# A norm's row factor multiplied after the products instead of before them, in a two-layer decoder step on one NeuronCore

## The chip, the cores and the metric

The kernel runs on one core of a Trainium2 chip. The time is the device time of one execution in microseconds (us). The engines named below are TensorE (PE, the matrix products; its weight loads are listed apart as PEld), VectorE (DVE), ScalarE (ACT), GpSimd (POOL) and SyncE (SP, which only issues transfers). ACT can issue transfers too, from a queue of its own.

## The reference, cut to what matters

One step of a decoder with two layers over 1024 prompt tokens and 8 sample tokens (1032 rows in all, d = 1024). Every layer is: norm, mixer, output projection plus residual, norm, feed-forward plus residual. Cut to what the change touches:

```python
def _rmsnorm(x, g):
    r = lax.rsqrt(jnp.mean(x * x, axis=-1, keepdims=True) + EPS)   # one factor per token (row)
    return x * r * g

# mixer A (layer 0): gate branch, RG-LRU input branch and memory queries
h = _rmsnorm(x, norm_mix_g);  z = h @ w_in_a
# output projection and residual, then the feed-forward
x = x + mix @ w_out
u = _rmsnorm(x, norm_ffn_g) @ w_ffn_up            # 1024 -> 6144: 24 pairs of 128 gate and 128 value columns
u = causal_conv3(u, state) + bias                 # along the tokens, samples from their own state
x = x + (gelu(u_gate) * u_value) @ w_ffn_down     # 3072 -> 1024
```

The norm's factor r is one number per token, so (x * g * r) @ w equals r * ((x * g) @ w).

## The kernel before, in words

Activations lie with features on the 128 partitions and tokens along the free axis. Every product is taken in three parts: both operands are split into a rounded part (hi) and a rest (lo), and `mm3` issues hi by hi, hi by lo and lo by hi. The hi comes from ACT (a copy, `acopy`, recorded at L105), the lo from a subtraction on DVE (`vtt`, L113) or on POOL (`gtt`, L116). Weights arrive on SP's queue, ACT makes hi, POOL makes lo (`get`, `w_split`), one tile ahead.

The tokens are cut into blocks of 384, 384 and 264 for the mixers and into four quarters of 258 (`QB`, `QW`) for the output projection and the feed-forward. The order on PE, DVE, POOL and SP is chosen by the Tile framework's scheduler; ACT keeps program order in layer 0 and in the feed-forward of layer 1.

In time the stages are: norm of the input and the first gate products (0 to 60 us), memory keys and queries, the RG-LRU stage (190 to 333), output projection 0 with the entry into the feed-forward (333 to 522), feed-forward up (522 to 985) and down (985 to 1245), mixer B, output projection 1 with its entry (1625 to 1785), up (1785 to 2246), down (to the end).

**Entry.** `x_norm(b)` squares the 8 feature tiles of a block, sums them with one product by `ones` each on PE (L565), takes Ln and Exp for r, and multiplies x by g and r before the split.

**Output projection.** `out_proj` goes over two halves of the tokens and in each over 8 feature tiles m: it loads the residual tile x[m] on SP (`residual`, L772), takes two quarters of 258 tokens in 24 products each, adds the result into x[m] on DVE, stores the sum to `rD` on SP (L1323), squares it on ACT and sums on DVE. After each half `norm` takes r of both quarters (`inverse`, product at L1335), multiplies all of x by g and r, and builds the differences T1 to T4 of the quarters for the feed-forward.

**Feed-forward up.** It is a Strassen-like scheme: for each pair of columns j, seven products P1 to P7 of 24 matmuls on each half of the tokens, 168 matmuls of 258 columns per j. POOL makes the combinations of the weights and their lo, ACT their hi; DVE adds the products into the row buffers ug and uv. `post(j)` then does for ug and uv: tap 2 and bias on ACT over 1032 columns, the last columns copied to `ul` on POOL (L867), two taps on DVE (L119) over 1023 and 1022 columns and an 8-column addition for the samples; then gelu on ACT, the product gate by value on DVE, and a store.

Of the kernel before, what the change touches and what calls it, by code (L numbers as in the profile page):

```python
# [34 lines left out]
QW = HALF // 2  # L35
QB = tuple(QW * q for q in range(4))
DCH = 6
NDC = KF // DCH
# [6 lines left out]
SEQUENCE = ENTRY + tuple((j, p, (0, 1)) for j in range(1, KF) for p in STEADY)  # L45
ORDER_A = ("g2", "g3", "x0", "x1", "x2", "x3", "x4", "x5", "g4", "g5")
# [3 lines left out]
def tile_trunk(ctx: ExitStack, tc: tile.TileContext, I: dict, O: list):  # L50
# [149 lines left out]
    def x_load(b):  # L200
        c0, n = BLK[b]
        per = 1024 // n if n > 264 else 3
        for k0 in range(0, KD, per):
# [3 lines left out]
            for j in range(m):  # L207
                X[b, k0 + j] = t[:, j * n : (j + 1) * n]

    x_load(0)  # L210
    pack = cst(PACK, "pack")
    ident = pack[:, 0:P]
# [340 lines left out]
    def unspill(k):  # L553
        t = row()
        SY.dma_start(t[:, :SEQ].rearrange("p (i t) -> p i t", i=8), xD[0:8, :, k, :].rearrange("i p t -> p i t"))
        SY.dma_start(t[:, SEQ:NT], xD[8, :, k, :NB])
        return t
# [132 lines left out]
    def sample_mem(l, dst):  # L690
# [35 lines left out]
        yield  # L726
        t = ps()
# [40 lines left out]
    def residual(l, m):  # L768
        if l:
            return unspill(m)  # L770
        t = row()
        SY.dma_start(t[:, :NT], I["x_t"][:, m, :])  # L772
        return t

    def out_proj(l, mget, ks, x, on_tile, on_half):
        for hb in range(2):
            for m in range(KD):
# [4 lines left out]
                for q in (2 * hb, 2 * hb + 1):  # L782
                    c0 = QB[q]
# [15 lines left out]
    def ffn_prep(l):  # L799
# [11 lines left out]
        vtt(s3, s3, c3, add)  # L811

# [45 lines left out]
    def ffn(l, x, ops, need, weights, on_block, store=None):  # L858
# [11 lines left out]
        def taps(a, u, t):  # L870
            stt(a[:, 1:SEQ], u[:, 0 : SEQ - 1], fwc(1, t), a[:, 1:SEQ], mul, add)
            stt(a[:, 2:SEQ], u[:, 0 : SEQ - 2], fwc(0, t), a[:, 2:SEQ], mul, add)
            vtt(a[:, SEQ:NT], a[:, SEQ:NT], sb3[:, :, t], add)

        def post(j):
# [9 lines left out]
            act(ag[:, :NT], ag[:, :NT], AF.Gelu_apprx_tanh)  # L885
            yield
            vtt(ag[:, :NT], ag[:, :NT], av[:, :NT], mul)
            SY.dma_start(gD[l, j], ag[:, :NT])
            yield

# [61 lines left out]

        last = []
        todo = [(0, p) for p in STEADY] + [(j, p) for j, p, _ in SEQUENCE if j]
        at = 7
        for q, (j, name, hfs) in enumerate(SEQUENCE):
            if q == 6:
                load_pair(1)
            want = 7 if q < 10 else min(len(todo), q - 7 + AHEAD)
# [51 lines left out]
        for b in range(3):  # L1011
            for m in range(KD):
                down(c, m, b)
                if store is not None:
                    store(m, b)
                tick()
            on_block(b)
# [4 lines left out]
    def x_norm(b):  # L1022
        n = BLK[b][1]
        xb = [X.pop((b, k)) for k in range(KD)]
        r = sm()
        yield from norm_r(xb, n, r[:, :n], b < 2)
        yield from norm_h(xb, b, r[:, :n], g_mix[0], hh, hl, True)

    load_w(1)
    SY.dma_start(pack, I["pack"])  # L1030
    x_load(1)
    load_w(2)
# [58 lines left out]
    def xr_dense(t, b):  # L1091
# [14 lines left out]
        def post():  # L1106
# [3 lines left out]
            acopy(u[:, 3 : 3 + n], p[:, :n])  # L1110
# [65 lines left out]
    def gt_dense(t, b):  # L1176
# [7 lines left out]
        if t == KR - 1:  # L1184
            act(M[t][:, cs], p[:, :n], AF.Gelu_apprx_tanh)
        else:
            acopy(M[t][:, cs], p[:, :n])
        if b == 2:
            drop(f"gt{t}")
            if t == KR - 1:  # L1190
                gelu_done.add(t)
            else:
                gelu_wait.append(t)
# [10 lines left out]
    x0 = start(x_norm(0))  # L1204
    ts(V, pack[:, 432:560], pack[:, 432:560], 0.125, None, mul, None)
    get("gt0", 0, 0)
    advance(x0)
    advance(x0)
    x1 = start(x_norm(1))
    finish(x0)  # L1210
    get("gt1", 0, 0)
    finish(x1)
    x2 = start(x_norm(2))
    for _ in range(3):
        advance(x2)
    tasks.remove(x2)
    gt_dense(0, 0)
    gt_dense(1, 0)
    gt_dense(0, 1)
    tasks.append(x2)  # L1220
    finish(x2)
    memt = start(mem_turn(mems))
    mems = None
    tasks.remove(memt)
    gt_dense(1, 1)
    gt_dense(0, 2)
    tasks.append(memt)
    gt_dense(1, 2)
# [23 lines left out]
    for i in range(9):  # L1252
# [10 lines left out]
        start(q_mem(0, p[:, :256], i, ready0) if i < 8 else q_sample(0, p[:NB, :256]))  # L1263
# [23 lines left out]
    SY.dma_start(O[1], yl)  # L1287
    SY.dma_start(O[2], rl)
# [21 lines left out]
    def enter_ffn(l, x, mh, ml):  # L1310
        ops, gen, sums = {}, {}, {}

        def split(name, kk, hf, pair, raw, on_pool):
            hi, lo = pair
            acopy(hi, raw)
            (gtt if on_pool else vtt)(lo, raw, f(hi), sub)
            ops[name, kk, hf] = pair

        def cols(q):
            return slice(QB[q], QB[q] + QW)  # L1320

        def on_tile(q, m):
            SY.dma_start(rD[l, m, :, cols(q)], x[m][:, cols(q)])  # L1323
            if m == 0:
                sums[q] = sm()
                act(sums[q][:, :QW], x[m][:, cols(q)], AF.Square)
            else:
                t = sm()
                act(t[:, :QW], x[m][:, cols(q)], AF.Square)
                vtt(sums[q][:, :QW], sums[q][:, :QW], t[:, :QW], add)  # L1330

        def inverse(q):
            a = sums.pop(q)
            p = ps()
            T.matmul(p[:, :QW], ones, a[:, :QW], start=True, stop=True)  # L1335
            m, out, t = sm()[:, :QW], sm()[:, :QW], sm()[:, :QW]
            ts(V, m, p[:, :QW], 1.0 / D, EPS, mul, add)
            act(out, m, AF.Ln)
            act(out, out, AF.Exp, scale=-0.5)
            stt(t, m, -0.5, out, mul, mul)  # L1340
            vtt(t, t, out, mul)
            stt(out, t, 1.5, out, add, mul)
            return out

        def norm(hf):
            qa, qb = cols(2 * hf), cols(2 * hf + 1)
            ra, rb = inverse(2 * hf), inverse(2 * hf + 1)
            yield
            xs = lambda k, part: x[k][:, part]

            def scale(k, part, r):
                stt(xs(k, part), xs(k, part), g_ffn[l][k], r, mul, mul)

            def slot(k, part):
                return mh[k][:, part], ml[k][:, part]

            def own(n):
                for i in range(n):
                    if i % 2 == 0:
                        t = row(F32R)  # L1360
                    b = (i % 2) * 2 * QW
                    yield t[:, b : b + QW], t[:, b + QW : b + 2 * QW]

            for k in range(KD):
                scale(k, qa, ra)
                split("B11" if k < 4 else "B21", k % 4, hf, slot(k, qa), xs(k, qa), k % 2)
                if k % 4 == 3:
                    yield
            t2 = own(4)
            for kk in range(4):  # L1370
                scale(kk, qb, rb)
# [620 lines left out]
```

## Time and profile before

| | us |
|---|---|
| median of 3 runs | 2532.33 (2530.51 to 2533.36) |
| the profiled execution's own time | 2532.97 |
| its span, first to last instruction | 2531.2 |
| PE busy | 2336.5 (92%) |
| DVE, ACT, POOL busy | 1549.6, 1103.5, 1428.0 |
| mean granted clock of PE | 0.964 |

Busy time of an engine holds what an instruction waits inside itself, once it has started. The idle time before an instruction names what was awaited last. A matmul's end is modelled, so the rate of PE is read from how many matmuls stand in a window rather than from one row.

### The profile page before, as it was taken

To read this page: it belongs to the slowest core of one execution; us is meant where nothing else is said; L and a number is where in the kernel's file an instruction comes from. 1 tells how busy PE (TensorE), PEld (TensorE's weight loads), DVE (VectorE), ACT (ScalarE), POOL (GpSimd) and SP (SyncE) were. 2 spreads that over 40 slices of the span, in tenths; PEclk is the share of its full clock that TensorE was granted. 3 is DMA by queue.
4 is the path that set the end of the run, shared out by engine and by line. 5 is a ranking of instruction groups with operands and counts; after the bars stand their busy time and mean duration, and the time that the engine had idled before them with its cause. 6 is when DMAs were issued, how large, how long until landed. Compare 5 with 4: busy or idle time off the path is not lost. (4 is left out here: it accounts for less than half of the span.)

```text
span 2531.2 us, 42857 instructions
## 1 busy us (share of the span) xinstructions
PE 2336.5 (92%) x16590; PEld 2251.5 (89%) x16590; DVE 1549.6 (61%) x2826; ACT 1103.5 (44%) x2277; POOL 1428.0 (56%) x1123
## 2 busy tenths in 40 slices
PE   7997877799999999999989988787999999999999
PEld 5896866799999999999977787677999999999999
DVE  6658955666666666332478789875666566663321
ACT  5567753344433444211365577643443444442110
POOL 2149843588888885322144346435888888853220
PEclk9998989899999999999999999899999999999999
DMA  4221124212222225421575543551222222253311
GB/s 163 87 69 56 58 83 143 63 67 84 84 85 76 76 76 199 150 95 52 178 252 162 185 152 129 163 157 63 77 86 82 76 76 76 76 224 123 101 55 63
DMA packets 142491, 273.64 MB, mean 108 GB/s; under 512 B 28544, under 2 KB 85456, under 8 KB 142288
## 3 DMA queue, kind: packets, MB, share of 16 engines
q1 hardware_dynamic: 142288, 270.91, 31.9%
q8 instruction: 130, 2.13, 0.3%
q14 instruction: 73, 0.60, 0.1%
HBM read 211.99 MB, written 58.87 MB: 107 GB/s over the span
## 5 line engine op out<-in xcount | busy, mean ns | idle before, releaser
L116 POOL TENSOR_TENSOR row<-row,row 128x512 fp32r<-128x512 f32 (+9 forms) x754 | 1153.8, 1552 | 793.9 <-ACT row L105 476.4
L298 PE MATMUL ps<-row,row 128*128 128x258 f32 (+4 forms) x5032 | 1510.4, 303 | 55.5 <-ACT row L105 45.7
L299 PE MATMUL ps<-row,row 128*128 128x258 f32 (+4 forms) x5032 | 1509.1, 302 | 22.5 <-DVE row L113 18.7
L300 PE MATMUL ps<-row,row 128*128 128x258 f32 (+4 forms) x5032 | 1472.7, 301 | 23.5 <-POOL row L116 23.5
L298 PEld LDWEIGHTS ps<-row,row 128*128 128x128 f32 x5032 | 962.3, 191 | 73.9 <-ACT row L105 51.0
L299 PEld LDWEIGHTS ps<-row,row 128*128 128x128 f32 x5032 | 964.0, 192 | 40.2 <-DVE row L113 24.3
L300 PEld LDWEIGHTS ps<-row,row 128*128 128x128 f32 x5032 | 948.4, 192 | 34.1 <-POOL row L116 27.1
L105 ACT ACTIVATE row<-row 128x512 fp32r<-128x512 f32 (+8 forms) x768 | 505.4, 696 | 911.7 <-POOL row L116 305.4
L113 DVE TENSOR_TENSOR row<-row,ps 128x258 f32<-128x258 f32 (+2 forms) x736 | 322.3, 444 | 706.0 <-PE ps L300 666.5
L119 DVE SCALAR_TENSOR_TENSOR row<-row,fw,row 128x1023 f32<-128x1023 f32 x192 | 266.9, 1409 | 67.3 <-ACT row L105 67.3
L113 DVE TENSOR_TENSOR row<-row,row 128x258 fp32r<-128x258 f32 (+8 forms) x262 | 232.9, 912 | 31.3 <-ACT row L105 18.0
L105 ACT ACTIVATE row<-ps 128x258 f32<-128x258 f32 (+6 forms) x430 | 157.5, 406 | 69.6 <-PE ps L300 25.8
L116 POOL TENSOR_TENSOR row<-row,ty 128x768 f32<-128x768 f32 (+2 forms) x56 | 77.2, 1378 | 155.1 <-DVE ty L413 51.3
L105 ACT ACTIVATE row<-row,fw 128x1032 f32<-128x1032 f32 x96 | 114.9, 1245 | 68.8 <-DVE row L113 68.7
L105 ACT ACTIVATE sm<-row 128x258 f32<-128x258 f32 (+3 forms) x130 | 54.5, 452 | 153.5 <-DVE row L113 127.2
L113 DVE TENSOR_TENSOR row<-row,sb 128x8 f32<-128x8 f32 x96 | 102.3, 1066 | 0.0
L113 DVE TENSOR_TENSOR sm<-sm,sm 128x258 f32<-128x258 f32 (+5 forms) x125 | 81.9, 660 | 28.2 <-ACT sm L105 25.7
L105 ACT ACTIVATE row<-ps,ty,ty 128x256 f32<-128x256 f32 (+1 forms) x160 | 87.4, 564 | 10.1 <-DVE ty L113 7.6
L105 ACT ACTIVATE sm<-ps 128x384 f32<-128x384 f32 (+5 forms) x156 | 65.0, 444 | 39.2 <-PE ps L431 21.6
L113 DVE TENSOR_TENSOR row<-ps,row 128x384 fp32r<-128x384 f32 (+2 forms) x125 | 63.5, 519 | 25.1 <-ACT row L105 10.2
L119 DVE SCALAR_TENSOR_TENSOR row<-sm,pack,row 128x384 f32<-128x384 f32 (+1 forms) x54 | 62.6, 1162 | 14.6 <-POOL row L124 13.3
L116 POOL TENSOR_TENSOR sm<-sm,row 128x192 f32<-128x192 f32 (+3 forms) x72 | 49.5, 702 | 36.1 <-ACT sm L105 18.6
(163 smaller groups left out, 1497.3 us busy)
## 6 DMA issues: line engine op xcount, KB each, us to landing
row<-in_w_ffn_up SPq DMA_DIRECT2D x96, 512.0 KB, 3.3
gD<-row SPq DMA_DIRECT2D x48, 516.0 KB, 2.6
row<-gD SPq DMA_DIRECT2D x48, 516.0 KB, 5.6
row<-in_w_ffn_down SPq DMA_DIRECT2D x64, 384.0 KB, 3.1
row<-hD SPq DMA_DIRECT2D x48, 512.0 KB, 6.6
row<-in_w_out SPq DMA_DIRECT2D x32, 512.0 KB, 4.2
rD<-row SPq DMA_DIRECT2D x64, 129.0 KB, 1.9
row<-rD SPq DMA_DIRECT2D x16, 516.0 KB, 8.7
```

The costliest lines, as they stand in the source:

```text
L105: return nc.scalar.activation(out, in_, func, **kw)
L113: return V.tensor_tensor(out=out, in0=a, in1=b, op=op)
L116: return G.tensor_tensor(out=out, in0=a, in1=b, op=op)
L119: return V.scalar_tensor_tensor(out=out, in0=a, scalar=s, in1=b, op0=op0, op1=op1)
L298: T.matmul(out, ah, bh, start=first and j == 0, stop=False, skip_group_check=more)
L299: T.matmul(out, ah, bl, start=False, stop=False, skip_group_check=more)
L300: T.matmul(out, al, bh, start=False, stop=last and j == n - 1, skip_group_check=more)
```

## The change

The row factor r leaves the operands of the products. At the entry, `x_split` splits x * g as it arrives, the products of the gate and the RG-LRU input start without r, and their results are multiplied by a row of r (`rA`) when DVE takes them from PSUM; the memory queries use columns of r. r itself (`x_factor`) is made beside the products with one product by `ones` per block, where there were eight. The first transfer is now the packed constants, then the first weights, then x.

In the output projection the residual is loaded in pairs of feature tiles ahead of use, the sum goes to a small buffer, its store is issued from ACT's queue, and `combine_x` builds T3, T2 and T4 and their splits inside the projection. `settle` splits the rest. `factor` makes r of the four quarters once the first ten products of the feed-forward have been issued, and keeps it in three buffers of 344 columns. `act_conv` multiplies ug and uv by these, three DVE instructions each, ahead of the taps. The samples' columns are left out of taps, gelu and product and done for 12 j's at a time in `samples`. Two more yields stand before the transposes of the samples' memory softmax, and two output stores come later.

```diff
+RW = NT // 3
+SG = 12
+TILES = (0, 4, 1, 5, 2, 6, 3, 7)
@@ def sample_mem
         ts(V, pt[:32, :256], pt[:32, :256], rd[:32, :1], None, mul, None)
         yield
+        yield
+        yield
@@ def out_proj
-            for m in range(KD):
+            for m in TILES:
                 key = f"out{l}.{hb}.{m}"
                 wh, wl = get(key, 1, 1)
-                if x[m] is None:
-                    x[m] = residual(l, m)
+                if m < 4:
+                    fetch()
...
-                    vtt(x[m][:, c0 : c0 + QW], x[m][:, c0 : c0 + QW], p[:, :QW], add)
-                    on_tile(q, m)
+                    on_tile(hb, part, m, p[:, :QW])
@@ def ffn
         def act_conv(u, t):
+            for i, r in enumerate(factor()):
+                cs = slice(i * RW, i * RW + RW)
+                vtt(u[:, cs], u[:, cs], r, mul)
             a = row()
-            act(a[:, :NT], u[:, :NT], AF.Identity, scale=fwc(2, t), bias=fbc(t))
+            act(a[:, :SEQ], u[:, :SEQ], AF.Identity, scale=fwc(2, t), bias=fbc(t))
             G.tensor_copy(out=ul3[:, :, t], in_=u[:, SEQ - 2 : NT])
...
-            vtt(a[:, SEQ:NT], a[:, SEQ:NT], sb3[:, :, t], add)
...
+            if j % SG == SG - 1:
+                samples(j - SG + 1)
@@ entry
+    def x_split(b):
+        for t, k0, m in X[b]:
+            for j in range(m):
+                k, xk = k0 + j, t[:, j * n : (j + 1) * n]
+                acopy(hh[k][:, cs], xk, scale=g_mix[0][k])
+                stt(hl[k][:, cs], xk, g_mix[0][k], f(hh[k][:, cs]), mul, sub)
@@ RG-LRU input branch
-            acopy(u[:, 3 : 3 + n], p[:, :n])
+            vtt(u[:, 3 : 3 + n], p[:, :n], rA[:, cs], mul)
@@ def gt_dense
-            acopy(M[t][:, cs], p[:, :n])
+            vtt(M[t][:, cs], p[:, :n], rA[:, cs], mul)
@@ def enter_ffn
-        def on_tile(q, m):
-            SY.dma_start(rD[l, m, :, cols(q)], x[m][:, cols(q)])
+        def on_tile(hf, part, m, p):
+            xs, t = place(hf, part, m), sm()
+            vtt(t[:, :QW], xs, p, add)
+            acopy(xs, t[:, :QW], scale=g_ffn[l][m])
+            nc.scalar.dma_start(rD[l, m, :, QB[q] : QB[q] + QW], t[:, :QW])
...
-        def norm(hf):
+        def combine_x(hf, kk):
+            vtt(t3, d, b, sub)
+            vtt(b, b, a, sub)
+            vtt(t2, d, b, sub)
+            vtt(t4, c, t2, sub)
...
+        def factor():
+            for q in list(sums):
+                inverse(q)
+            return rf
```

The names in the following rows are buffers: row and sm are buffers in SBUF, ps is PSUM, fw holds the taps, sb the samples' state part, ul the saved columns. First DVE in the steady part of the feed-forward up of layer 0, before: the last products of one j are added, then come the taps.

```order
L113 TENSOR_TENSOR row_7258<-row_7258,ps_7332 128x258
L113 TENSOR_TENSOR row_7258<-row_7258,ps_7345 128x258
L119 SCALAR_TENSOR_TENSOR row_7419<-row_7258,fw,row_7419 128x1023
L113 TENSOR_TENSOR row_7419<-row_7419,sb 128x8
L119 SCALAR_TENSOR_TENSOR row_7425<-row_7222,fw,row_7425 128x1023
L113 TENSOR_TENSOR row_7425<-row_7425,sb 128x8
L119 SCALAR_TENSOR_TENSOR row_7419<-row_7258,fw,row_7419 128x1022
L119 SCALAR_TENSOR_TENSOR row_7425<-row_7222,fw,row_7425 128x1022
```

The same place on DVE now; sm_4935 to sm_4937 are the three buffers of the row factor.

```order
L116 TENSOR_TENSOR row_7249<-row_7249,sm_4935 128x344
L116 TENSOR_TENSOR row_7249<-row_7249,ps_7271 128x258
L116 TENSOR_TENSOR row_7284<-row_7284,ps_7358 128x258
L116 TENSOR_TENSOR row_7249<-row_7249,sm_4936 128x344
L116 TENSOR_TENSOR row_7249<-row_7249,sm_4937 128x344
L116 TENSOR_TENSOR row_7284<-row_7284,sm_4935 128x344
L116 TENSOR_TENSOR row_7284<-row_7284,sm_4936 128x344
L116 TENSOR_TENSOR row_7284<-row_7284,ps_7371 128x258
L116 TENSOR_TENSOR row_7284<-row_7284,sm_4937 128x344
L122 SCALAR_TENSOR_TENSOR row_7448<-row_7284,fw,row_7448 128x1023
L122 SCALAR_TENSOR_TENSOR row_7456<-row_7249,fw,row_7456 128x1023
```

Six multiplications of 344 columns, with both inputs in SBUF, stand between the additions of products and the taps; the two additions of 8 columns are gone. On POOL one j's work between the copies to ul was, before:

```order
L867 COPY ul<-row_7222 128x10
L116 TENSOR_TENSOR row_7058<-row_7058,row_7060 128x512
L116 TENSOR_TENSOR row_7329<-row_7326,row_7329 128x512
L116 TENSOR_TENSOR row_7360<-row_7058,row_7360 128x512
L116 TENSOR_TENSOR row_7390<-row_7058,row_7390 128x512
L116 TENSOR_TENSOR row_7326<-row_7058,row_7326 128x512
L867 COPY ul<-row_7258 128x10
L116 TENSOR_TENSOR row_7428<-row_7326,row_7428 128x512
```

And now on POOL:

```order
L895 COPY ul<-row_7249 128x10
L119 TENSOR_TENSOR row_7416<-row_7080,row_7416 128x512
L895 COPY ul<-row_7284 128x10
L119 TENSOR_TENSOR row_7459<-row_7352,row_7459 128x512
L119 TENSOR_TENSOR row_7591<-row_7321 128x512
L119 TENSOR_TENSOR row_7494<-row_7082,row_7494 128x512
L119 TENSOR_TENSOR row_7529<-row_7352,row_7529 128x512
```

The two copies have moved together, with one weight operation between them, and each reads a buffer that the multiplications write. On SP's queue in output projection 0, before:

```order
L251 DMA row_3496<-in_w_out 128x1024
L1287 DMA out<-yl 128x54
L772 DMA row_3498<-in_x_t 128x1032
L1323 DMA rD<-row_3498 128x258 x2
L251 DMA row_3599<-in_w_out 128x1024
L772 DMA row_3601<-in_x_t 128x1032
L1323 DMA rD<-row_3601 128x258 x2
```

And now on SP, from the same projection's first residual on:

```order
L786 DMA row_3447<-in_x_t 128x2x516
L254 DMA row_3453<-in_w_out 128x1024
L786 DMA row_3455<-in_x_t 128x2x516
L847 DMA row_3492<-in_w_ffn_up 128x1024
L847 DMA row_3494<-in_w_ffn_up 128x1024
```

The stores to rD no longer stand between the loads; one residual load serves two feature tiles, and the first feed-forward weights come before most of the projection's.

## Rows read from the trace of the kernel before

**Rows 1.** Windows by stage: us; busy and count of PE, PEld, DVE, ACT, POOL; clock; DMA.

```profile
333.00:522.00 189.00, 138.65 (x947) 130.31 (x948) 109.45 (x205) 67.88 (x153) 91.15 (x68) 0.84 0.31 98
522.00:985.00 463.00, 460.65 (x3827) 460.06 (x3827) 298.33 (x391) 195.97 (x324) 390.88 (x296) 1.00 0.23 82
...
1625.00:1785.00 160.00, 131.67 (x950) 124.62 (x949) 109.06 (x221) 64.44 (x142) 80.10 (x63) 0.89 0.41 127
1785.00:2246.00 461.00, 458.98 (x3812) 458.48 (x3812) 290.63 (x388) 195.26 (x323) 383.97 (x294) 1.00 0.23 81
```

**Rows 2.** Window inside the feed-forward up, layer 0.

```profile
600.00:650.00 50.00, 50.00 (x418) 50.00 (x417) 31.19 (x41) 22.07 (x36) 44.03 (x36) 1.00 0.18 64
```

**Rows 3.** Timeline of POOL, feed-forward up: start, duration, operation.

```profile
699.51 2.53 POOL L116 TENSOR_TENSOR row<-row,row 128x512 fp32r<-128x512 f32 x2
...
709.52 2.29 POOL L116 TENSOR_TENSOR row<-row,row 128x512 fp32r<-128x512 f32 x1
```

**Rows 4.** Groups by form, 600 to 940 us: shapes, count, busy, mean ns, idle before.

```profile
L116 POOL TENSOR_TENSOR row<-row,row 128x512 fp32r<-128x512 f32 x119 | 187.4, 1593 | 50.7 <-ACT row L105 50.7
...
L116 POOL TENSOR_TENSOR row<-row,row 128x512 f32<-128x512 f32 x51 | 82.7, 1622 | 0.0
...
L113 DVE TENSOR_TENSOR row<-row,ps 128x258 f32<-128x258 f32 x169 | 69.9, 421 | 102.6 <-PE ps L300 102.1
...
L113 DVE TENSOR_TENSOR row<-row,sb 128x8 f32<-128x8 f32 x34 | 42.8, 1260 | 0.0
...
L116 POOL TENSOR_TENSOR row<-row 128x512 f32<-128x512 f32 x17 | 22.0, 1295 | 0.0
...
L113 DVE TENSOR_TENSOR row<-row,row 128x1032 f32<-128x1032 f32 x17 | 20.8, 1222 | 0.0
```

**Rows 5.** Timeline of DVE, the same stretch.

```profile
708.19 1.26 DVE L113 TENSOR_TENSOR row<-row,sb 128x8 f32<-128x8 f32 x1
709.38 1.27 DVE L119 SCALAR_TENSOR_TENSOR row<-row,fw,row 128x1023 f32<-128x1023 f32 x1
```

**Rows 6.** Timeline of DVE, end of the RG-LRU stage.

```profile
336.96 0.14 DVE L113 TENSOR_TENSOR row<-row,pack 128x8 f32<-128x8 f32 x1
```

**Rows 7.** Timeline of DVE, output projection 0.

```profile
366.21 0.76 DVE L113 TENSOR_TENSOR row<-row,ps 128x258 f32<-128x258 f32 x2 [5.96 <-DMA row<-in_x_t]
367.13 0.77 DVE L113 TENSOR_TENSOR sm<-sm,sm 128x258 f32<-128x258 f32 x2 [0.15 <-ACT sm L105]
373.33 0.76 DVE L113 TENSOR_TENSOR row<-row,ps 128x258 f32<-128x258 f32 x2 [5.43 <-DMA row<-in_x_t]
```

**Rows 8.** Timeline of SP's queue, output projection 0.

```profile
366.67 0.80 SPq L1323 DMA_DIRECT2D rD<-row  x2
...
368.01 0.45 SPq L772 DMA_DIRECT2D row<-in_x_t  x1
```

**Rows 9.** Waits of PE, 330 to 530 us.

```profile
PE ps L298 <- ACT row L105: 26.7, 10, 8.2
```

**Rows 10.** Timeline of PE, entry.

```profile
4.93 7.31 PE L565 MATMUL ps<-sm,ones 128*128 128x384 f32 x13 [4.93 <-ACT sm L105]
...
20.35 0.63 PE L298 MATMUL ps<-row,row 128*128 128x384 f32 x1
```

**Rows 11.** The page's transfers: count, KB each, us to landing.

```profile
row<-in_w_ffn_up SPq DMA_DIRECT2D x96, 512.0 KB, 3.3
```

**Rows 12.** Waits of PE, 0 to 100 us: total, times, longest.

```profile
PE ps L299 <- DVE row L113: 9.1, 3, 4.5
```

**Rows 13.** Window in the RG-LRU stage.

```profile
240.00:250.00 10.00, 0.00 (x0) 0.00 (x0) 9.92 (x16) 8.18 (x13) 9.12 (x7) 0.50 0.41 125
```

**Rows 14.** Timeline of PE, the samples' softmax transposes.

```profile
250.01 0.42 PE L729 MATMUL ps<-pack,sm 32*128 32x32 f32 x2 [12.59 <-DVE sm L123]
```

**Rows 15.** Timeline of ACT, output projection 0.

```profile
366.67 0.75 ACT L105 ACTIVATE sm<-row 128x258 f32<-128x258 f32 x2 [5.01 <-DVE row L113]
367.33 1.04 ACT L105 ACTIVATE row<-row 128x1024 fp32r<-128x1024 f32 x1
```

More of the change, by code (lines that the diff above doesn't have):

```diff
@@ L1202, in gelus @@
         gelu_wait.clear()
-    x0 = start(x_norm(0))
+    held = []
+    get("gt0", 0, 0)
     ts(V, pack[:, 432:560], pack[:, 432:560], 0.125, None, mul, None)
[L1206 to L1210, printed above, removed]
-    get("gt1", 0, 0)
[L1212 to L1221, printed above, removed]
+    x_split(0)
+    f0 = start(x_factor(0))
+    gt_dense(0, 0, held)
+    get("gt1", 0, 0)
+    x_split(1)
+    gt_dense(1, 0, held)
+    advance(f0)
+    f1 = start(x_factor(1))
+    gt_dense(0, 1, held)
+    for e in held[:2]:
+        e()
+    del held[:2]
+    x_split(2)
+    finish(f0)
+    gt_dense(1, 1, held)
+    advance(f1)
+    f2 = start(x_factor(2))
+    gt_dense(0, 2, held)
     memt = start(mem_turn(mems))
     mems = None
[L1224 to L1228, printed above, removed]
+    for e in held[:2]:
+        e()
+    del held[:2]
+    finish(f1)
+    gt_dense(1, 2, held)
+    advance(f2)
+    advance(memt)
+    for e in held:
+        e()
+    finish(f2)
     finish(memt)
@@ L1310, in enter_ffn, with split @@
     def enter_ffn(l, x, mh, ml):
[L1311 to L1314 removed]
+        ops, gen, sums, own, wait = {}, {}, {}, {}, []
+        rf = []
+        def split(name, kk, hf, hi, lo, raw):
             acopy(hi, raw)
[L1316 to L1320, printed above, removed]
[L1322 to L1323 removed]
+            vtt(lo, raw, f(hi), sub)
+            ops[name, kk, hf] = hi, lo
@@ L1327, in on_tile @@
             else:
-                t = sm()
-                act(t[:, :QW], x[m][:, cols(q)], AF.Square)
-                vtt(sums[q][:, :QW], sums[q][:, :QW], t[:, :QW], add)
+                s = sm()
+                act(s[:, :QW], t[:, :QW], AF.Square)
+                vtt(sums[q][:, :QW], sums[q][:, :QW], s[:, :QW], add)
+            if part == 0 and wait:
+                combine_x(*wait.pop())
+            if part == 1 and m >= 4:
+                wait.append((hf, m - 4))
+        def combine_x(hf, kk):
+            a, b = place(hf, 0, kk), place(hf, 1, kk)
+            c, d = place(hf, 0, kk + 4), place(hf, 1, kk + 4)
+            t3, t2, t4 = (sm()[:, :QW] for _ in range(3))
+            vtt(t3, d, b, sub)
+            vtt(b, b, a, sub)
+            vtt(t2, d, b, sub)
+            vtt(t4, c, t2, sub)
+            for name, t in (("T3", t3), ("T2", t2), ("T4", t4)):
+                if kk % 2 == 0:
+                    own[name] = row(F32R)
+                o = (kk % 2) * HALF
+                split(name, kk, hf, own[name][:, o : o + QW], own[name][:, o + QW : o + HALF], t)
@@ L1332, in inverse @@
         def inverse(q):
+            if not rf:
+                rf.extend(sm()[:, :RW] for _ in range(3))
             a = sums.pop(q)
@@ L1406, in first_pair @@
                 yield
+        gen["w"] = spawn(first_pair())
         def on_half(hf):
+            if wait:
+                combine_x(*wait.pop())
             if hf:
                 finish(gen["w"])
-            gen[hf] = start(norm(hf))
-            if not hf:
-                gen["w"] = spawn(first_pair())
+            gen[hf] = start(settle(hf))
         def need(name, kk, hf):
```

252 lines of the change are left out of this document (149 added, 103 removed).

## The prediction

> **What bounds the kernel now.** I read the page's busy times first, then windows by stage, then in each stage the groups, the waits and the timeline of the engine that PE waits for.
>
> The two feed-forward up stages are bound by PE: it is busy 460.65 of 463 us and 458.98 of 461 [rows 1]. Inside, every us of a 50 us window is filled and the granted clock is 1.00, the 2.4 GHz level [rows 2]. A j is 168 matmuls; 418 in 50 us make 20.1 us for one j, and the 463 us of a stage are 23 such periods. But POOL, which makes the weights for the next products, is busy 44.03 of the 50 [rows 2], and the reader should see that much of this is waiting: its 128x512 operation takes 1.27 us where two stand in 2.53, and 2.29 in another place [rows 3], with a mean of 1.59 [rows 4]. DVE shows the other side of it: an addition on 8 columns takes 1.26 us there, 1.26 in the mean of 34 [rows 4, 5], and 0.14 at the end of the RG-LRU stage [rows 6]. An 8-column operation that lasts as long as one POOL operation is one that stood behind it. The additions that read PSUM and one SBUF buffer show nothing of this: 0.421 us in the mean of 169 [rows 4]. So DVE operations with two SBUF inputs and POOL operations take turns in this stage, the others not.
>
> The Trainium skill states this as a rule (SBUF — State Buffer, "Who interferes with whom"): a DVE instruction with two SBUF inputs contends with a GpSimd instruction that reads SBUF, the pair is an exclusive lock, and one SBUF input does not contend. The trace agrees, with the 1.26 against 0.14 us and the 0.421 us above. It speaks against this change, whose multiplications in the feed-forward have two SBUF inputs; by it they cost what the first term below says, and without it nothing.
>
> The two output projections are not bound by PE: 138.65 busy of 189 us and 131.67 of 160 [rows 1]. In layer 0 the tile's period is 373.33 less 366.21, 7.1 us, and DVE waits 5.43 of it for the residual [rows 7]. That load is issued on SP behind the stores of the tile before, which go out at 366.67 when that tile's sums are done [rows 8], and behind a weight load. So the loop is: sums, stores, loads, 5 us of transfer, sums. PE needs 48 matmuls, at the rate above 5.8 us. Over the whole stretch PE waits 26.7 us for ACT [rows 9], mostly where the norm's splits stand between projection and feed-forward.
>
> **The change part by part.** The sum is made against the profiled execution, 2533.0 (span 2531.2 and 1.8 around it); the median of the runs, 2532.3, lies 0.7 below, which I neglect.
>
> *Multiplications in the feed-forward up.* What takes turns, per j before: 11 POOL operations ((119 + 51 + 17) / 17 [rows 4]) of 1.27 us [rows 3], 13.9; four taps of 1.27 [rows 5], 5.1; the product of 1032 columns, 1.22 [rows 4]; two of 8 columns at 0.14 [rows 6], 0.3. Together 20.5, against a period of 20.1. Printed durations hold a little before and after the part that excludes, so I read this as: the turns fill the period already, and PE is only just the bound. Added are six multiplications of 128x344. The nearest rows are 0.77 for two of 258 columns with two SBUF inputs [rows 7], 0.51 by width, and a third of 1.22 for 1032 columns [rows 4], 0.41; I take 0.45, so 2.7 us, less 0.3 for the removed 8-column additions: 2.4 us per j. The samples' five small POOL operations come once in 12 j and I cost them at nothing, since 48 eight-column additions go for them. Over 23 periods in each of two layers: +110 us. The bounds: 0, if what really excludes is 2.4 us shorter per j than printed (the removed additions give nothing back below that, PE being full); and above, 50.7 us of POOL's idle over 17 j, 3.0 each [rows 4], which taps fill today. The copies to ul now stand behind the multiplications and the weights behind the copies; if only one tap of 1.27 still finds that gap, 1.7 more is lost, 4.1 per j, +190.
>
> *Entry.* The first gate product starts at 20.35, behind 16 products by ones that begin at 4.93 [rows 10]. Now it needs x, one ACT copy and one DVE operation per tile, as the first square did, plus the constants and a 512 KB weight tile that are now loaded ahead; such a tile lands in 3.3 us [rows 11]. That makes 8, so 12 us sooner. The 9.1 us of waits for DVE's splits [rows 12] I expect to remain in another place, and one of them to shorten by 1: -13, between -5 (if DVE's splits and r's chain hold the next products) and -20 (all of it and the waits).
>
> *RG-LRU input branch and gate results.* 18 evictions go from ACT to DVE. They read PSUM and one SBUF buffer, the 0.42 us form of 258 columns [rows 4], 0.5 to 0.6 at 384, so 9 us of DVE in a stage in which DVE is busy 9.92 of 10 us and PE waits [rows 13]. ACT gets the same time back, at 8.18 of 10. I take +5, from -8 to +12. The transposes that stall PE for 12.59 us [rows 14] get two yields; PE's work then goes ahead of them, but DVE stays full and the next product is late instead: 0 within the same bounds.
>
> *Output projection and entry into the feed-forward.* The residual is loaded ahead and the stores leave SP, so the loop of 7.1 us falls. What is next is PE's 5.8 and ACT, which now has per tile two copies, two store issues, two squares and the hi of the next weights: 4 times 0.375, 1.04 [rows 15], and two issues at SP's price of 0.40 each [rows 8], 3.3 us, in order. So 1.3 us for 8 tiles, 10 us in layer 0's first half. The larger part is the norm, no longer ahead of the splits: PE's work in the 189 us is 768 and 168 matmuls, 112 us at the full rate, and 77 are lost. The start of the projection (some 14, behind the RG-LRU stage) stays; of the other 63 I let half go, 35 us with the 10 in it. In layer 1, 48 of 160 are lost, and I let 25 go. Sum -60, between -30 (only the loop and one norm) and -95 (three quarters of all but the start).
>
> The down stages, mixer B and the memory attention keep their instructions: 0.
>
> Sum: 2533 + 110 - 13 + 5 - 60 = **2575 us**.
>
> **Rivals.**
>
> *The multiplications are hidden (faster).* DVE is busy 31.19 of 50 us [rows 2], so its own time suffices: 12.5 per j and 2.7 more. If the exclusive part is clearly shorter than the printed durations, PE stays the bound at 20.1. For it: PE shows no wait in the stage although the printed turns exceed the period. Against: the 1.26 us of eight columns. It gives 2533 - 13 + 5 - 60 = 2465 us. The point from which the kernel is slower is 68 / 46 = 1.5 us per j.
>
> *Half of it is hidden.* The turns cost 1.2 per j, 55 us: 2520 us, and anything from 2500 to 2545 with the other terms' bounds.
>
> *ACT becomes the bound of the output projection (slower).* In its order the hi of the next weights stands behind copy, store issue and square of the tile before, and POOL's lo behind that; if it comes later than the 5.8 us of PE, the tile keeps its 7 us, and the gain there is 15 instead of 60. With the turns at 2.8 per j (130): 2533 + 130 - 13 + 5 - 15 = 2640 us.
>
> *The change doesn't do what it says:* r is still waited for. If r's chain, now in the feed-forward's first j, holds back the first multiplications, the row buffers of j 0 stay filled and PE waits once per layer, some 10 us each: it shifts the forecast to 2595 and is inside its range.
>
> **How the numbers follow.** Forecast (2545 to 2610) 0.5; hidden 0.2; half 0.18; ACT the bound 0.12. A measurement can tell 0.2%, 5 us, from no change. Hidden is faster; of half, 0.12 faster, 0.03 within, 0.03 slower; of the forecast 0.02 faster, 0.03 within, 0.45 slower; the last is slower. So faster 0.34, same 0.06, slower 0.60. The range for 8 in 10 is 2462 to 2640: it takes in the middle of the hidden case and that of the last; the forecast's own is the 2545 to 2610 above.
>
> **What would show it.** In the feed-forward up: fewer matmuls per 50 us than 418 (374 at 22.5 us per j), PE waiting for POOL's or ACT's weights, multiplications of 344 columns with a mean well over 0.5 us. If instead 418 stays and the multiplications take 0.4 to 0.5 us, the turns were not full and the first term is wrong. At the entry the first product near 8 us. In the projection, tiles at 5.3 to 6.5 us and no wait for the residual; tiles still at 7 us with ACT full would be the third rival. The prediction is wrong as a whole if up stages stay under 1.5 us of loss per j.

## The result and the profile after

The changed kernel takes 2631.1 us (median of 4, 2627.66 to 2636.2) where the kernel before takes 2531.4: a ratio of 1.0394, with a 95% interval from 1.0372 to 1.0417. It is slower, as forecast, but by 99.7 us and not by 42. The time lies inside the range of 2462 to 2640, close to its upper end, and outside the forecast's own 2545 to 2610.

The spans of the two profiled executions differ by 94.6 us (2625.8 less 2531.2). The start of the first product of each stage, read from PE's list of matmuls, cuts this into pieces:

| stretch | before, us | after, us | difference | forecast |
|---|---|---|---|---|
| start to the first product of output projection 0 | 335.3 | 329.0 | -6.3 | -13 + 5 |
| from there to the end of the feed-forward's j 0, layer 0 | 186.4 | 150.4 | -36.0 | -35 |
| the same in layer 1 | 169.0 | 155.4 | -13.6 | -25 |
| j 1 to j 23, layer 0 | 468.7 | 536.7 | +68.0 | +55 |
| j 1 to j 23, layer 1 | 469.1 | 535.9 | +66.8 | +55 |
| down of layer 0 and mixer B | 624.5 | 637.1 | +12.6 | 0 |
| down of layer 1 to the end | 278.2 | 281.3 | +3.1 | 0 |

The windows of the changed kernel that answer to [rows 1] and [rows 2] come first. The columns are those of [rows 1]. The first pair are the two output projections, the second pair the feed-forward up.

```profile
329.00:449.00 120.00, 104.25 (x771) 100.44 (x772) 91.69 (x144) 63.52 (x136) 68.21 (x38) 0.91 0.40 124
...
1653.00:1782.00 129.00, 105.03 (x810) 102.53 (x808) 90.87 (x174) 67.25 (x147) 59.65 (x35) 0.90 0.52 158
```

```profile
600.00:650.00 50.00, 45.68 (x364) 45.06 (x362) 37.24 (x46) 17.89 (x29) 36.82 (x30) 0.97 0.18 64
650.00:700.00 50.00, 44.21 (x351) 43.80 (x352) 37.07 (x45) 19.11 (x33) 36.34 (x27) 0.97 0.21 74
```

PE was busy 50 of 50 us; now it is busy 44 to 46, with 351 to 364 matmuls where 418 stood. From the start of j 2 to the start of j 23 a period (from the first product of one j to that of the next) is 20.2 us in the mean before and 23.1 after, in both layers. POOL is not busier than before: it is less busy, because its work has been stretched over more time.

The mean clock of 0.97 hides whole drops. In 15 of these 42 periods the granted clock stands for 3.41 us at 0.50, the 1.2 GHz level; before, in none. Two neighbouring periods, and the wait of PE just ahead of the drop in the second, which begins at 674.88:

```profile
643.68:666.34 22.66, 20.43 (x170) 20.23 (x169) 17.08 (x22) 8.39 (x14) 17.74 (x14) 1.00 0.19 71
666.34:690.59 24.25, 21.99 (x171) 21.79 (x169) 17.15 (x22) 8.39 (x14) 17.81 (x14) 0.93 0.20 66
```

```profile
674.51 0.39 PE L301 MATMUL ps<-row,row 128*128 128x258 f32 x1 [2.26 <-ACT row L108]
```

Counted over PE's list of matmuls and the granted clock, the 15 periods with a drop take 24.23 us in the mean, the 14 right behind one 22.17, and the 13 others, with no drop in them or in the one before, 22.72. In the first and the last kind PE is idle for the same 2.3 us; with a drop its products take 1.5 us longer. Measured against the 22.72 the drops add 15 us to these 42 periods, and against the mean of all 27 without one (22.44) 27 us.

The groups of the same stage show where it goes (600 to 900 us; shapes, count, busy, mean ns, idle before):

```profile
L119 POOL TENSOR_TENSOR row<-row,row 128x512 fp32r<-128x512 f32 x91 | 140.3, 1560 | 34.9 <-ACT row L108 34.9
L116 DVE TENSOR_TENSOR row<-row,sm 128x344 f32<-128x344 f32 x78 | 79.4, 1056 | 0.9
...
L108 ACT ACTIVATE row<-row 128x512 fp32r<-128x512 f32 x91 | 54.3, 622 | 110.2 <-POOL row L119 110.2
...
L122 DVE SCALAR_TENSOR_TENSOR row<-row,fw,row 128x1022 f32<-128x1022 f32 x26 | 45.6, 1792 | 0.0
L122 DVE SCALAR_TENSOR_TENSOR row<-row,fw,row 128x1023 f32<-128x1023 f32 x26 | 32.4, 1286 | 18.7 <-ACT row L108 17.2 <-POOL sm L119 1.4
```

The multiplication of 344 columns lasts 1.06 us in the mean, twice its price by width. (The tap of 1.79 us has no part in the loss: it takes 1.70 and 1.77 us in two kernels below whose period is 20.2.) An instruction that waits for its turn, that is, for the other engine's operation to end, shows the wait as its own duration. The timelines of DVE and then POOL (start, duration, operation, count):

```profile
712.26 4.04 DVE L116 TENSOR_TENSOR row<-row,sm 128x344 f32<-128x344 f32 x4
...
716.66 1.15 DVE L116 TENSOR_TENSOR row<-row,sm 128x344 f32<-128x344 f32 x1
719.26 5.90 DVE L122 SCALAR_TENSOR_TENSOR row<-row,fw,row 128x1023 f32<-128x1023 f32 x4 [1.44 <-ACT row L108]
```

```profile
703.62 11.88 POOL L119 TENSOR_TENSOR row<-row,row 128x512 fp32r<-128x512 f32 x8
715.43 0.50 POOL L895 COPY ul<-row 128x10 f32<-128x10 f32 x1
...
717.88 0.20 POOL L895 COPY ul<-row 128x10 f32<-128x10 f32 x1 [0.44 <-DVE row L116]
720.88 2.00 POOL L119 TENSOR_TENSOR row<-row,row 128x512 fp32r<-128x512 f32 x1 [2.80 <-ACT row L108]
```

Four multiplications take 4.04 us, and eight POOL operations 11.88. Taken singly, the POOL operation beside additions that read PSUM lasts 1.29 us, near the 1.27 of [rows 3]; one between two multiplications lasts 1.58, and the multiplication behind it 1.62:

```profile
711.14 1.29 POOL L119 TENSOR_TENSOR row<-row,row 128x512 fp32r<-128x512 f32 x1
713.92 1.58 POOL L119 TENSOR_TENSOR row<-row,row 128x512 f32<-128x512 f32 x1
714.25 1.62 DVE L116 TENSOR_TENSOR row<-row,sm 128x344 f32<-128x344 f32 x1
```

What PE waits for in the stage (560 to 960 us; total, times, longest) is the hi of the next weights from ACT, whose copies stand idle 110.2 us for POOL in the groups above:

```profile
PE ps L301 <- ACT row L108: 36.6, 17, 2.8
```

The entry answers to [rows 10]: the first product starts at 7.23 and no product by ones stands ahead of it.

```profile
7.23 0.69 PE L301 MATMUL ps<-row,row 128*128 128x384 f32 x1 [7.23 <-ACT row L108]
8.86 0.69 PE L302 MATMUL ps<-row,row 128*128 128x384 f32 x1 [0.94 <-DVE row L122]
```

In output projection 0 DVE's additions, which stood 7.1 us per tile apart waiting for the residual [rows 7], no longer wait for it (each is one quarter, two make a tile):

```profile
367.54 0.42 DVE L116 TENSOR_TENSOR sm<-row,ps 128x258 f32<-128x258 f32 x1
...
370.64 0.42 DVE L116 TENSOR_TENSOR sm<-row,ps 128x258 f32<-128x258 f32 x1 [0.34 <-PE ps L303]
...
374.01 0.41 DVE L116 TENSOR_TENSOR sm<-row,ps 128x258 f32<-128x258 f32 x1
```

From 367.54 to 374.01 a tile takes 6.5 us. PE's waits for ACT in this projection (330 to 449 us) are small now, and most of its waiting is for POOL:

```profile
PE ps L303 <- POOL row L119: 8.3, 6, 3.0
PE ps L302 <- DVE row L116: 4.4, 4, 1.8
PE ps L301 <- ACT row L108: 2.8, 3, 1.8
```

In layer 1 a new wait stands at the start of the second half. PE's row and SP's rows before it:

```profile
1732.82 1.23 PE L301 MATMUL ps<-row,row 128*128 128x258 f32 x4 [13.87 <-ACT row L108]
```

```profile
1700.17 0.45 SPq L564 DMA_DIRECT2D row<-xD  x1
1709.12 0.37 SPq L565 DMA_DIRECT2D row<-xD  x1
...
1720.85 0.48 SPq L568 DMA_DIRECT2D row<-xD  x1
1724.92 3.96 SPq L1919 DMA_DIRECT2D row<-mD  x8
```

The loads of the mixer's last token block (row<-mD), which the second half's products need, are issued at 1724.92, behind the residual loads (row<-xD) of that half, which trickle out over 20 us.

### The profile page after: what moved, and what is told of

The parts are those of the page before. It is cut to its first block, busy times and chain, and to the rows that moved or that the text cites. A ratio compares the mean times of both kernels' runs of the same rounds, so it can differ in the third digit from the quotient of the medians.

```text
span 2625.8 us, 43084 instructions
## 1 busy us (share of the span) xinstructions
PE 2344.8 (89%) x16571; PEld 2262.1 (86%) x16571; DVE 1775.5 (68%) x3006; ACT 1112.3 (42%) x2285; POOL 1412.3 (54%) x1091
## 4 chain that ended last, share of the span: by engine, by line
PE 56%; DVE 23%; ACT 9%; issue 5%; POOL 4%; DMA 3%; SPq 0%; ACTq 0%; DVEq 0%; POOLq 0%
PE ps L301 18%; PE ps L302 18%; PE ps L303 17%; DVE row L116 13%; ACT row L108 7%; DVE row L122 3%; POOL row L119 3%; DVE sm L116 2%; ACT sm L108 1%; DVE ty L116 1%; DVE row L1245 1%; DVE ty L399 1%; DVE sm L122 0%; DVE ty L122 0%; DMA row<-in_cache_mem_k 0%
## 5 line engine op out<-in xcount | busy, mean ns | idle before, releaser
L119 POOL TENSOR_TENSOR row<-row,row 128x512 fp32r<-128x512 f32 (+8 forms) x702 | 1093.8, 1582 | 719.3 <-ACT row L108 422.4
L108 ACT ACTIVATE row<-row 128x512 fp32r<-128x512 f32 (+10 forms) x681 | 482.5, 745 | 868.2 <-POOL row L119 390.9
L116 DVE TENSOR_TENSOR row<-row,ps 128x258 f32<-128x258 f32 (+2 forms) x672 | 295.1, 446 | 546.5 <-PE ps L303 538.2
L116 DVE TENSOR_TENSOR row<-row,sm 128x344 f32<-128x344 f32 x288 | 273.7, 987 | 4.0 <-DVE row L116 0.5
L116 DVE TENSOR_TENSOR row<-row,row 128x1024 f32<-128x1024 f32 (+10 forms) x186 | 226.7, 1234 | 33.4 <-ACT row L108 25.4
L108 ACT ACTIVATE row<-row,fw 128x1024 f32<-128x1024 f32 x96 | 113.9, 1234 | 170.9 <-DVE row L116 170.9
L108 ACT ACTIVATE row<-ps 128x258 f32<-128x258 f32 (+4 forms) x412 | 149.6, 404 | 69.6 <-PE ps L303 21.0
L119 POOL TENSOR_TENSOR row<-row 128x512 f32<-128x512 f32 x48 | 88.2, 1838 | 90.6 <-PE ps L303 82.8
L116 DVE TENSOR_TENSOR row<-ps,row 128x384 fp32r<-128x384 f32 (+3 forms) x143 | 72.0, 516 | 22.3 <-ACT sm L108 7.3
L108 ACT ACTIVATE sm<-ps 64x384 f32<-64x384 f32 (+5 forms) x138 | 57.3, 445 | 57.9 <-PE ps L434 39.7
```

The lines of the kernel that those rows point to most:

```text
L108: return nc.scalar.activation(out, in_, func, **kw)
L116: return V.tensor_tensor(out=out, in0=a, in1=b, op=op)
L119: return G.tensor_tensor(out=out, in0=a, in1=b, op=op)
```

## The experiments

The main theory: DVE instructions with two SBUF inputs take turns with POOL's in the feed-forward up, and six more turns per j are what costs. The rivals: the chain through the multiplications got longer (copies to ul, taps and weights come later whatever the operands); or other edits of the feed-forward did it.

**The multiplications left out.** Edit: the loop `for i, r in enumerate(factor())` of `act_conv` is gone, so the row factor is missing from the result.

> The changed kernel without the six multiplications of a j in the feed-forward up (the row factor is still made, but left out of the rows). If the multiplications are what lengthens a j from 20.2 to 23.1 us, a j falls back to 20.2 to 20.4 us and the kernel from 2631 to about 2500 us (46 periods of 2.9 us less). If the lengthening came from the changed operand splits, the tap order or the copies to ul, a j stays at 22 us or more and the kernel above 2570 us.

Measured: 2494.3 us, ratio to before 0.9853 (0.9834 to 0.9871). A j is back at 20.2 us. From j 1 to the end of j 23 the two layers take 470.0 and 469.2 us, where the changed kernel takes 536.7 and 535.9 and the kernel before 468.7 and 469.1. So the multiplications are the whole loss of this stage, and the rest of the change is worth some 38 us.

**The row factor in PSUM.**

```diff
-            for i, r in enumerate(factor()):
-                cs = slice(i * RW, i * RW + RW)
-                vtt(u[:, cs], u[:, cs], r, mul)
+            for i in range(2):
+                cs = slice(i * 512, i * 512 + 512)
+                vtt(u[:, cs], u[:, cs], factor()[i], mul)
...
-                rf.extend(sm()[:, :RW] for _ in range(3))
+                rf.extend(ps() for _ in range(2))
+                rf.append(sm())
...
+                z = ul3[:, 2:10, t0 : t0 + SG]
+                gtt(z, z, factor()[2][:, 0:8, None].to_broadcast([P, 8, SG]), mul)
```

> The changed kernel with the row factor kept in PSUM (two buffers of 512 columns, so four multiplications of 512 in place of six of 344; the samples' 8 columns are multiplied on POOL, once in 12 j). The multiplications stand in the same place of the order, but have one SBUF input only. Theory of turns: they no longer alternate with POOL, cost 0.5 to 0.7 us each, a j falls to 20.2 to 20.6 us and the kernel to 2500 to 2520 us. Rival, the chain through the multiplications (copies to ul and taps come later): a j stays at 22.5 us or more, the kernel at 2600 us or more. Two PSUM buffers fewer for the products could cost 0 to 0.5 us per j.

Measured: 2497.8 us, 0.9861 (0.9844 to 0.9879), 2 us below the expected band. The multiplications are all there, and cost next to nothing: 3.5 us separate it from the kernel without them, and a j takes 20.2 us. The window and the group of this kernel:

```profile
600.00:650.00 50.00, 50.00 (x419) 50.00 (x418) 33.85 (x48) 21.32 (x35) 39.31 (x34) 1.00 0.18 64
```

```profile
L116 DVE TENSOR_TENSOR row<-row,ps 128x512 f32<-128x512 f32 x60 | 38.5, 684 | 3.1
```

PE is full again. 512 columns take 0.68 us where 344 took 1.06. This decides against the longer chain.

**The multiplications alone, added to the kernel before,** with a buffer of ones, first in SBUF and then in PSUM (there the buffer is called `hold[0]`). Edit for both, in `act_conv`:

```diff
+            for i in range(3):
+                cs = slice(i * 344, i * 344 + 344)
+                vtt(u[:, cs], u[:, cs], one[:, :344], mul)
             a = row()
```

> The kernel before with six multiplications by ones of 344 columns per j, both inputs in SBUF, at the place where the changed kernel has them. Nothing else is changed. Theory of turns: a j goes from 20.2 to 22.5 to 23.5 us, the kernel to 2640 to 2680 us. Rival, the other edits of the feed-forward (no sample columns in the taps, samples in groups of 12) made it slow: a j stays below 21 us, the kernel below 2570 us.

> The kernel before with the same six multiplications by ones of 344 columns as before_mult, but with the ones in a PSUM buffer. Theory of turns: a j stays at 20.2 to 20.4 us (3.17 us less than before_mult) and the kernel at 2530 to 2545 us. Rival, DVE's added time or the longer chain costs: a j over 21.5 us, the kernel over 2590 us.

Measured: 2676.6 us with SBUF, 1.0565 (1.0542 to 1.0588); 2541.4 with PSUM, 1.0044 (1.0031 to 1.0058). A j takes 23.37 and 20.17 us, 20.21 before. A window (600 to 650 us) and the group of each of the two kernels, SBUF first:

```profile
600.00:650.00 50.00, 45.64 (x355) 45.23 (x356) 39.42 (x50) 17.48 (x31) 36.43 (x27) 0.94 0.18 64
L113 DVE TENSOR_TENSOR row<-row,sm 128x344 f32<-128x344 f32 x78 | 76.7, 1022 | 0.9
```

```profile
600.00:650.00 50.00, 50.00 (x418) 50.00 (x417) 37.97 (x58) 22.40 (x36) 44.09 (x34) 1.00 0.18 64
L113 DVE TENSOR_TENSOR row<-row,ps 128x344 f32<-128x344 f32 x90 | 40.7, 508 | 2.4 <-ACT row L105 0.5
706.29 1.32 POOL L116 TENSOR_TENSOR row<-row,row 128x512 fp32r<-128x512 f32 x1
```

The same operation on the same columns: 1.02 us with the second input in SBUF, 0.51 with it in PSUM. The last row is a POOL operation during which three multiplications of the PSUM form start: at 1.32 us it is hardly held up. Nothing else of the change is needed to make the feed-forward slow. The 11 us that the PSUM form still adds are not in its j's (within 0.1 us in the mean); 6.8 of the 9.7 us between the two spans lie in the stretch of mixer B, of which more below.

The clock drops here too: in 18 of the 42 periods from j 2 to j 22. These take 24.95 us in the mean, the 16 behind one 21.70, the 8 others 23.14.

**Half as many.** As the SBUF form, for the gate half only (`range(3 if t < KF else 0)`).

> The kernel before with three of the six multiplications by ones per j (those of the gate half only). It asks whether the turns were full before: six cost 3.17 us per j. If full, three cost half, 1.4 to 1.7 us per j, and the kernel is at 2600 to 2612 us. If there was slack of s in a j of 20.2 us, six cost 6c - s and three 3c - s: three would cost under 1.2 us per j, the kernel below 2590 us.

Measured: 2593.9 us, 1.0245 (1.0228 to 1.0261), between the two bands. A j takes 21.56 us: three cost 1.35, six 3.17. The window of 600 to 650 us and PE's waits from 560 to 960:

```profile
600.00:650.00 50.00, 47.85 (x397) 47.44 (x396) 33.65 (x47) 18.48 (x33) 40.33 (x31) 1.00 0.23 83
PE ps L298 <- ACT row L105: 19.8, 18, 1.2
```

PE waits 1.0 to 1.3 us once per j, and the clock stays at 1.00 from j 2 to j 22; with six it waits 2.6 us or more in 26 of the 42 periods, and the clock drops. So the two costs can't be compared as they stand. If each turn costs c and the period had a slack s, 6c - s = 3.17 and 3c - s = 1.35 give c = 0.61 and s = 0.47 us. With the periods of the six that hold no drop and follow none (23.14, so 2.93) c is 0.53 and s 0.24. Both are estimates, two numbers from two periods: the turns were nearly full, not quite.

**Fewer, longer turns,** in the kernel before and in the changed one: the factor in one SBUF buffer of 1032 columns, `vtt(u[:, :NT], u[:, :NT], r[:, :NT], mul)`.

> The kernel before with the same multiplication by ones, but as one instruction of 1032 columns per row buffer (two per j, two SBUF inputs) in place of three of 344. If a turn's price is its columns (0.61 us for 344), two cost 6 times 0.61 less the 0.47 of slack, 3.2 us per j, and the kernel stays at 2670 to 2680 us. If each turn has a price of its own beside its columns, two long ones cost 2 times 1.15 to 1.25 less 0.47, 1.8 to 2.1 us per j, and the kernel is at 2615 to 2632 us.

> The changed kernel with the row factor in one SBUF buffer of 1032 columns, so one multiplication per row buffer (two per j) in place of three of 344. Before, the same replacement took a j from 23.4 to 22.2 us. If the number of turns is what the small buffers cost here too, a j falls from 23.1 to 21.7 to 22.2 us and the kernel from 2631 to 2570 to 2590 us. Rival: without the 8-column additions and with the copies to ul behind the long multiplications nothing is gained; a j stays over 22.7 us, the kernel over 2610 us.

Measured: 2622.6 us before, 1.0365 (1.0349 to 1.038); 2558.4 in the changed kernel, 1.0108 (1.0092 to 1.0124), better than expected. A j takes 22.17 and 21.67 us, where 20.21 and 20.20 stood. The clock stays at 1.00 in every one of these periods but one. With the slack of 0.24 two turns of 1032 columns cost 1.96 + 0.24, 1.10 each, where three of 344 cost 1.59; with 0.47 they cost 1.21 and 1.83. So by this estimate a turn has a price of 0.25 to 0.3 us beside its columns. The first pair of values gives back the changed kernel, with its two removed additions as two turns of 0.25: 2.4 us for six of 344 columns and 1.5 for two of 1032, where its periods without drops show 2.5 (22.72) and 1.4 (21.59). No run separates that price from what the clock does to the periods around a drop. Their windows, kernel before and then changed kernel (600 to 650 us):

```profile
600.00:650.00 50.00, 47.56 (x384) 46.27 (x384) 37.55 (x46) 19.63 (x34) 42.86 (x29) 1.00 0.25 95
```

```profile
600.00:650.00 50.00, 48.30 (x393) 47.27 (x393) 36.47 (x42) 19.89 (x34) 48.03 (x31) 1.00 0.27 96
```

The changed kernel is 73 us slower with the small buffers (2631.1 less 2558.4). Some 60 of these are in j 1 to j 23 (536.7 and 535.9 us with small buffers, 509.3 and 503.5 with the long one), the drops of the clock among them.

**The place in SP's queue.** Edit: `start_m(2)`, which issues the loads of the last block, is called at the fifth tile of the first half of output projection 1.

```diff
+                if hb == 0 and m == 2 and early is not None:
+                    early()
                 if m < 4:
                     fetch()
```

> The changed kernel with the loads of the third token block of the mixer's results in layer 1 asked for earlier, ahead of most residual loads on the same queue. Theory: the 13.9 us in which PE waits at the start of the second half of output projection 1 are a place in the queue; they go, and the kernel gets 8 to 14 us faster (2617 to 2623). Rival: the queue is full anyway or its waits only move; the time stays within 4 us.

Measured: 2619.1 us, 1.0343 (1.0327 to 1.0358); 12 us less than the changed kernel. The first half of that projection took 65.6 us before, 79.6 in the changed kernel and 65.7 here. PE's waits for ACT in the two halves fall from 20.8 to 12.3 us:

```profile
PE ps L301 <- ACT row L108: 12.3, 3, 8.1
```

The wait of 13.9 at the start of the second half is gone. The 8.1 stands early in the first half (1665.9 us), where the changed kernel has one of 6.9; a wait of 3.7 is new in the second half. From the projection's first product to the end of j 0 layer 1 takes 147.4 us here and 155.4 in the changed kernel, so 8 of the 12 us are in this stretch.

**Both mended,** and from there two parts of the change undone, one at a time: the added yields, and the stores on ACT's queue (`SY.dma_start(rD...)` in place of `nc.scalar.dma_start`).

> The changed kernel with both edits that helped it: row factor in PSUM, and the mixer's third block in layer 1 loaded ahead of the residuals. If the two losses are independent, their gains (133 and 12 us) add: 2486 us, with the second half of output projection 1 starting some 66 us after the first and a j at 20.2. If the place in the queue only paid off while POOL and DVE were late anyway, 2498 us.

> As psum_l1, without the two added yields before the softmax transposes of the sample memory attention. Theory (the yields cost in mixer B, where before no long stall stood): mixer B loses 4 to 10 us less, the RG-LRU stage gets the 12.6 us stall of PE back, of which at most 5 us reach the end; net 0 to 5 us faster than psum_l1. Rival: the yields pay for themselves in the RG-LRU stage, and without them the kernel is 3 to 8 us slower.

> As psum_l1, with the stores of the residual issued by SP again. Theory (the stores on SP held back the loads): with the residual loaded ahead the tiles need it less, but weight loads wait behind stores that wait for DVE; the two output projections get 5 to 20 us longer together. Rival: prefetching the residual alone was what mattered, or ACT's issues cost as much; within 4 us of psum_l1.

Measured: 2488.8 us, 0.9826 (0.9813 to 0.984), for both mended; 2486.0, 0.9815 (0.98 to 0.983), without the yields; 2487.5, 0.982 (0.9806 to 0.9834), with the stores on SP. The three can't be told apart. Each beats both kernels, by 45 to 48 us against before. Of the 2486 and 2498 us expected for both mended the gains that add are nearer; for the stores the rival holds, and the 5 to 20 us of the theory are not there. Neither the yields nor ACT's queue is worth anything measurable here.

**The eviction of the RG-LRU branch.** Edit: `acopy(u[:, 3 : 3 + n], p[:, :n])` in place of the multiplication by rA, so this branch lacks its row factor.

> As psum_ny, with the eviction of the RG-LRU input branch back on ACT and without its row factor (left out of that branch). Theory: DVE, full in that stage, gets 18 evictions of 0.5 us back, and output projection 0 starts 4 to 9 us sooner; the kernel at 2477 to 2482 us. Rival: the stage waits for the chain on POOL and ACT, and the change there is under 3 us.

Measured: 2478.4 us, 0.9797 (0.9781 to 0.9814), against 0.9815 (0.98 to 0.983) with the multiplication: 4.6 us by the ratios, with intervals that overlap. In the traces output projection 0 starts at 328.4 us and at 332.0 with the multiplication, but it starts anywhere from 327.7 to 331.6 in the kernels that share the changed kernel's code up to there. So the time of the kernel fits the 5 us of the forecast, and a gain is not shown.

## Why the prediction was right in direction and wrong in size

**The multiplications: mechanism right, the clock left out.** The term "2.4 us per j" gave +110, and the j's from 1 on lost 134.8 (68.0 and 66.8); of the three terms that missed, this one missed by most, 25 us. The price itself stands: a period without a drop of the clock, behind one without, takes 22.72 us, 2.5 more than before. The step that failed is that the term took PE's granted clock to stay at the 1.00 of [rows 2]. In the changed kernel PE waits 1.5 to 2.8 us once per j, and in 15 of 42 periods the clock falls to 0.50 for 3.41 us; that adds 15 us (27 by the other measure). Some 5 more are 42 times 0.1 of price, and 5 are j 1 and j 23: j 1, a period of 20.5 and 20.4 us, now takes 27.1 and 25.6, but 24.6 also without the multiplications. PE waits 6.6 and 4.6 us for ACT there; whether r's chain has a part in it, the fourth rival, is not shown. The account of the clock is read from the traces; no run holds the clock and changes nothing else.

That 2.4 came out so near is partly luck. By the estimates above a turn of 344 columns costs 0.53 us, not 0.45; 0.24 per period were free, so that "the turns fill the period already" was nearly right and not quite; and the two removed additions give back some 0.5, not 0.3. The upper end of this term, +190, was not reached, though one part of its reason shows: the copies to ul wait 9.0 us for the multiplications in 600 to 900 us, 0.7 per j, and not at all with the row factor in PSUM.

**Entry and RG-LRU stage: right in sum.** The first product starts at 7.23, forecast 8. The memory products start at 48.5 us in place of 63.9, 15.4 sooner where 13 was forecast; 9.1 of it are lost again before the output projection, where 5 was forecast, within its bound of 12. That it is the evictions that lose them is not shown. PE's stall at the softmax transposes was 12.59 us [rows 14] and they no longer wait; a wait of 7.0 for DVE stands at L774 in the same stage, and others have grown: the gap moved, as written, and taking the yields out changed nothing that can be measured.

**Output projection: right in layer 0, too hopeful in layer 1.** In layer 0 the loop over the residual is gone and the norm no longer stands ahead of the splits: -36.0 against -35 (half of the 63 us that the working starts from would be 31.5). The first half of the projection gives 8.8 of it, the second half with the norm 22.8, j 0 the rest, and PE's waits for ACT, 26.7 us in the projection with its entry [rows 9], are 2.8 in the projection and 1.1 in j 0. That "the stores leave SP" had a part in it is not shown: with the residual loaded ahead, the stores on SP again cost nothing. In layer 1 the -25 became -13.6. Of a step that was moved I had not followed what it is moved ahead of: the residual loads of the second half now stand ahead of the mixer's results on the same queue, and PE waits 13.9 us for these. Putting them first gave 12 us back, 8 of them in this stretch. The third rival, ACT as the bound, is wrong: a tile takes 6.5 us, ACT is busy 63.52 of 120 us there, and PE waits 8.3 us for POOL and 2.8 for ACT.

**Unchanged stages: not at 0.** Mixer B and the down stages took 15.7 us more, put at 0 because their instructions stay. What of this belongs to the change stays open. Mixer B with the down stage ahead of it took 624.5 us before, and in the four kernels that only add multiplications to the feed-forward up, with the same code for mixer B, 624.7, 630.1, 631.3 and 635.0. So up to 10 us come and go there without an edit in it. Taking out the yields shortened the stretch from 633.2 to 630.3, which is within that.

Summed up: of the 53 us between the forecast's 42 and the spans' 94.6, 25 are the multiplications' term (15 to 27 of it the clock), 11 layer 1's projection with its queue, 16 the stages that I took as unchanged. That the time still lies in the range is luck: the upper end, 2640, is the middle of the rival with ACT as the bound, which did not happen. The rivals in which the multiplications are hidden, wholly or by half, are ruled out by the kernel before with nothing but the multiplications added.

## What to carry to other kernels

Look at which operands an added DVE operation reads before pricing it: with POOL busy all the time, a second SBUF input made the same multiplication cost a turn in the alternation, and moving nothing but the buffer of ones to PSUM made 135 us of loss vanish (2676.6 against 2541.4). If it has to stay in SBUF, try few long instructions; one of 1032 columns in place of three took 73 us off the changed kernel and 54 off the kernel before with ones. When an engine that was full begins to wait, look whether PE's granted clock still holds: a mean of 0.97 was whole stretches at half the clock. And when loads are moved ahead, list what they now stand in front of on that queue.

## What the runs showed of the hardware

DVE operations with two SBUF inputs and POOL operations held each other up: a multiplication of 344 columns took 1.02 to 1.06 us in the mean, and a POOL operation between two of them 1.58 in place of 1.29. With one of the two inputs in PSUM the same instruction took 0.51 us in the mean of 90, beside a POOL as busy as before, and the period stayed at 20.2 us. A turn cost an estimated 0.53 to 0.61 us for 344 columns and 1.10 to 1.21 for 1032, in periods that were otherwise nearly full. PE's granted clock held at 1.00 while PE waited 1.0 to 1.3 us once per j (three multiplications) or mostly 0.6 twice (two long ones, kernel before). With six multiplications PE waited once per j, 2.2 us or more in two periods of three, and the clock fell to 0.50, the 1.2 GHz level, for 3.41 us or twice that in 15 and 18 of 42 periods; in the changed kernel a period with such a drop took 1.5 us longer.
